# Issuing the later loads of x from ScalarE instead of SyncE in an RMSNorm + matmul kernel

## The chip, the cores and the metric

The kernel runs on one core of one Trainium2 chip. The metric is the device time of the whole kernel in microseconds (us), lower is better. The profiled span is about 2 us shorter than the time.

## The reference

```python
# x (16, 1024, 512) f32, weight (512, 768) f32, gamma (512,) f32, out (16, 1024, 768) f32
rms = np.sqrt(np.mean(x ** 2, axis=-1, keepdims=True) + eps)
return np.matmul(x / rms * gamma, weight)
```

The 16,384 rows are worked on as 128 tiles of 128 rows, in 64 pairs.

## The kernel before

Each tile of x is loaded in f32, cast to bf16 by GpSimd, transposed by TensorE (f32 words that hold two bf16), copied out of PSUM by VectorE and multiplied with the weights. ScalarE takes the sum of squares, and the result is scaled by 1/rms as it leaves PSUM: the first tile of a pair by ScalarE, the second by VectorE. Then it is stored. Two input buffers of 16 tiles and three output buffers of 8 tiles are used in turn.

```python
xin  = ctx.enter_context(tc.tile_pool(name="xin", bufs=2))    # 16 tiles each
outp = ctx.enter_context(tc.tile_pool(name="out", bufs=3))    # 8 tiles each
opsum = ctx.enter_context(tc.tile_pool(name="opsum", bufs=3, space=bass.MemoryType.PSUM))
# ... cut ...
def load(i):
    if i // XG not in x_tiles:
        x_tiles[i // XG] = xin.tile([P, XG, D], F32, name="xt")
    nc.sync.dma_start(out=held(x_tiles, XG, i, x_size[i]), in_=rows(x, i, x_size[i]))

def store(i):
    first, n = o_first[i], o_size[i]
    if i == first + n - 1:
        nc.sync.dma_start(out=rows(out, first, n), in_=held(o_tiles, OG, first, n))
# ... cut ...
for j in range(2, NP):
    load_until(2 * j + AHEAD)                  # AHEAD = 20 tiles
    if j + 3 < NP:
        cast(2 * j + 6, nc.gpsimd, 2)
    # ... squares of pair j + 2 on ScalarE, transposes of pair j + 2 fed between the matmuls ...
    for i, engine in ((2 * j, nc.scalar), (2 * j + 1, nc.vector)):
        a = accumulator()
        matmuls(i, a, range(K), feed)
        finish_tile(i, a, engine)              # scale into the output buffer, then store(i)
```

Loads of x and stores thus share SyncE's queue, in program order.

## Time and profile before

| | before |
|---|---|
| time, median of 3 | 211.08 us (210.78 to 211.16) |
| profiled span | 209.0 us |
| PE / ACT / VectorE / GpSimd busy | 96% / 72% / 52% / 32% |
| moved by DMA | 85.69 MB |
| pace of the matmuls from pair 6 on | 3.037 us a pair |

"Busy" is the share of the span.

### The profile page before, as it was taken

What the parts mean: (1) busy time and instruction counts of PE and PEld (TensorE: products, weight loads), DVE (VectorE), ACT (ScalarE), POOL (GpSimd) and SP (SyncE); (2) the same over time, 40 slices, a digit from 0 to 9 for tenths busy, and PEclk for the clock granted to TensorE, in tenths of its full rate; (3) what the DMA queues carried; (4) which work ended last, traced back from release to release, by engine and by line L of the source; (5) the groups of instructions that cost most, each with busy time, mean ns of one, the idle gap of its engine ahead of it and who ended that gap; (6) DMA issues with size and microseconds to landing.
All of it is one profiled execution on the core that took longest, in us unless ns stands there. A gap on an engine that the chain in (4) does not pass through costs nothing.

```text
span 209.0 us, 3534 instructions
## 1 busy us (share of the span) xinstructions
PE 201.6 (96%) x1298; PEld 137.9 (66%) x1298; DVE 109.0 (52%) x173; ACT 149.6 (72%) x359; POOL 67.0 (32%) x73
## 2 busy tenths in 40 slices
PE   7999999999999999999999999999999999999980
PEld 2466777666766776667766776667667766677640
DVE  0465654654565465456545644654564465456550
ACT  2689987787778778777877777787777778777640
POOL 1357532306331073213623062310633045230000
PEclk9999999999999999999999999999999999999999
DMA  6999999999999999999999999999999999899994
GB/s 231 392 430 422 408 395 436 424 414 439 431 458 411 412 442 425 447 411 437 428 448 419 423 423 442 433 433 417 428 442 447 405 441 414 381 386 386 383 374 182
DMA packets 7077, 85.69 MB, mean 410 GB/s; under 512 B 786, under 2 KB 916, under 8 KB 3476
## 3 DMA queue, kind: packets, MB, share of 16 engines
q1 hardware_dynamic: 7056, 85.46, 97.0%
q8 instruction: 10, 0.16, 0.3%
q14 instruction: 7, 0.06, 0.1%
q10 hardware_dynamic: 4, 0.00, 0.0%
HBM read 35.13 MB, written 50.33 MB: 409 GB/s over the span
## 4 chain that ended last, share of the span: by engine, by line
PE 91%; ACT 3%; DMA 2%; POOL 1%; DVE 1%; issue 0%; SPq 0%
PE ops L168 77%; PE tp L133 13%; DMA xt<-in_x_dram 2%; ACT jk L98 1%; ACT ot L150 1%; POOL xb L94 1%; ACT rms L102 0%; DVE xT L140 0%; PE ops L227 0%; DVE ot L152 0%; SPq L206 0%; DVE rstd L104 0%
## 5 line engine op out<-in xcount | busy, mean ns | idle before, releaser
L168 PE MATMUL ops<-w_bf,xT 128*128 128x256 bf16 (+1 forms) x1024 | 194.2, 326 | 0.3 <-DVE xT L140 0.3
L168 PEld LDWEIGHTS <-xT 128*128 128x128 bf16 x1024 | 100.0, 98 | 56.4 <-DVE xT L140 1.4
L94 POOL CAST xb<-xt 128x1024 bf16<-128x1024 f32 (+1 forms) x67 | 66.3, 1002 | 118.9 <-PE tp L133 72.9
L150 ACT ACTIVATE ot<-ops,rstd 128x768 f32<-128x768 f32 (+1 forms) x65 | 58.1, 894 | 47.2 <-PE ops L168 47.2
L140 DVE COPY xT<-tp 128x1024 bf16<-128x1024 bf16 (+1 forms) x67 | 44.7, 667 | 83.3 <-PE tp L133 83.0
L98 ACT ACTIVATE jk<-xt 128x512 bf16<-128x512 f32 x128 | 78.7, 619 | 0.7 <-DMA xt<-in_x_dram 0.7
L133 PE MATMUL tp<-ident_f,xb 128*128 128x128 f32 x256 | 68.9, 273 | 0.1
L152 DVE TENSOR_SCALAR ot<-ops,rstd 128x768 f32<-128x768 f32 (+1 forms) x65 | 64.5, 993 | 2.9 <-PE ops L168 2.9
L133 PEld LDWEIGHTS tp<-ident_f,xb 128*128 128x128 f32 x256 | 35.9, 141 | 3.8 <-POOL xb L94 0.7
L98 ACT ACTIVATION_READ_ACCUMULATOR jk<-xt 128x1 f32 x128 | 24.4, 191 | 0.0
L102 ACT ACTIVATE rms<-ssq,eps_sb 128x4 f32<-128x4 f32 (+3 forms) x35 | 10.4, 297 | 1.1
L104 DVE RECIPROCAL rstd<-rms 128x4 f32<-128x4 f32 (+3 forms) x35 | 5.9, 167 | 3.3 <-ACT rms L102 3.3
L227 PE MATMUL ops<-warm 128*128 128x512 bf16 x16 | 6.4, 561 | 1.2 <-DVE eps_sb L220 1.2
L227 PEld LDWEIGHTS <-warm 128*128 128x128 bf16 x16 | 1.9, 131 | 3.9 <-issue 2.5
L150 ACT ACTIVATE w_bf<-w_f,g_sb 128x768 bf16<-128x768 f32 x2 | 1.9, 936 | 3.6 <-DMA w_f<-in_weight_dram 3.6
L201 ACT ACT_TABLE_LOAD x1 | 1.3, 1283 | 1.3 <-PEq L330 1.3
L152 DVE TENSOR_SCALAR w_bf<-w_f,g_sb 128x512 bf16<-128x512 f32 (+2 forms) x3 | 1.4, 485 | 1.1 <-DMA w_f<-in_weight_dram 1.0
L241 DVE COPY g_sb<-tp 128x4 f32<-128x4 f32 x1 | 0.2, 162 | 3.1 <-PE tp L239 3.1
L239 PEld LDWEIGHTS tp<-ident_f,g_row 2*128 2x128 f32 x2 | 0.3, 200 | 0.8 <-issue 0.8
L218 DVE MEMSET warm<- 128x256 uint32 x1 | 0.3, 272 | 0.9 <-PEq L330 0.9
L239 PE MATMUL tp<-ident_f,g_row 2*128 2x2 f32 x2 | 0.4, 264 | 0.0
masks.py:199 POOL TENSOR_SCALAR_AFFINE_SELECT ident_f<-ident_f 128x128 f32<-128x128 f32 x1 | 0.3, 292 | 0.1
(6 smaller groups left out, 0.7 us busy)
## 6 DMA issues: line engine op xcount, KB each, us to landing
out_dram<-ot SPq DMA_DIRECT2D x12, 3072.0 KB, 16.3
xt<-in_x_dram SPq DMA_DIRECT2D x5, 4096.0 KB, 23.0
xt<-in_x_dram SPq DMA_DIRECT2D x3, 2048.0 KB, 19.4
out_dram<-ot SPq DMA_DIRECT2D x4, 1536.0 KB, 11.6
xt<-in_x_dram SPq DMA_DIRECT2D x4, 1024.0 KB, 13.2
out_dram<-ot SPq DMA_DIRECT2D x4, 768.0 KB, 10.4
out_dram<-ot SPq DMA_DIRECT2D x7, 384.0 KB, 11.2
w_f<-in_weight_dram SPq DMA_DIRECT2D x2, 768.0 KB, 5.9
```

The source lines that it names most:

```text
L94: engine.tensor_copy(out=xb_tiles[i // 2][:, i % 2:i % 2 + n, :], in_=held(x_tiles, XG, i, n))
L98: nc.scalar.activation(out=jk, in_=held(x_tiles, XG, i)[:, 0, :], func=AF.Square, accum_out=ssq)
L102: nc.scalar.activation(out=rms[:, :n], in_=ssq[:, :n], func=AF.Sqrt, scale=1.0 / D, bias=eps_sb)
L104: nc.vector.reciprocal(out=rstd[:, :n], in_=rms[:, :n])
L133: nc.tensor.transpose(out=tp_tiles[j][:, t, h, :], in_=words[:, lo:lo + P], identity=ident_f)
L140: nc.vector.tensor_copy(out=dst[:, t:t + n, :], in_=src[:, t:t + n, :])
L150: nc.scalar.mul(out=dst, in_=src, mul=r)
L152: nc.vector.tensor_single_scalar(out=dst, in_=src, scalar=r, op=mybir.AluOpType.mult)
L168: nc.tensor.matmul(out=acc[:, lo:hi], lhsT=xT_tiles[i // 2][:, i % 2, k // 2, :, k % 2], rhs=w_bf[:, k, lo:hi], start=(k == 0), stop=(k == ...
L201: nc.scalar.preload_act_table(AF.Sqrt)
L227: nc.tensor.matmul(out=spare[:, :WIDE], lhsT=warm[:, :P], rhs=warm, start=True, stop=True)
L239: nc.tensor.transpose(out=gp[:, c, :], in_=g_row[:, :, c], identity=ident_f[:2, :2])
```

## The change

The intent is that loads and stores no longer stand behind each other in one queue: the loads from tile 32 on (two of 2048 KB, five of 4096 KB) are issued by ScalarE on its own queue, stores stay on SyncE's.

```diff
-        nc.sync.dma_start(out=held(x_tiles, XG, i, x_size[i]), in_=rows(x, i, x_size[i]))
+        queue = nc.sync if i < 2 * XG else nc.scalar
+        queue.dma_start(out=held(x_tiles, XG, i, x_size[i]), in_=rows(x, i, x_size[i]))
```

## The prediction

> **What bounds the kernel now.** I read the page of the kernel before first: busy shares, chain, costliest groups. The span is 209.0 us.
>
> ```profile
> PE 201.6 (96%) x1298; PEld 137.9 (66%) x1298; DVE 109.0 (52%) x173; ACT 149.6 (72%) x359; POOL 67.0 (32%) x73
> ...
> q1 hardware_dynamic: 7056, 85.46, 97.0%
> ...
> PE 91%; ACT 3%; DMA 2%; POOL 1%; DVE 1%; issue 0%; SPq 0%
> ...
> L168 PE MATMUL ops<-w_bf,xT 128*128 128x256 bf16 (+1 forms) x1024 | 194.2, 326 | 0.3 <-DVE xT L140 0.3
> ```
>
> The chain that ended last is 91% PE, and the matmuls of L168 waited 0.3 us in all. In the trace a new pair of tiles starts every 3.037 us from pair 6 (27.72 us) to pair 62 (197.78 us), without a break. So TensorE sets the end. But one queue, q1, is busy for 97% of the span: I had to ask how close the transfers are to taking over.
>
> In the steady part, 8 pairs take 8 x 3.037 = 24.3 us and need one load of 4096 KB and two stores of 3072 KB (the page's DMA issues): 4.194 + 2 x 3.146 = 10.49 MB, or 432 GB/s. Each transfer reports one completion for each of 16 DMA engines, and the last of the 16 counts. For the big loads that last one is at 72.72, 97.28, 121.53, 145.71 and 169.93 us: the last gaps are 24.25, 24.18 and 24.22 us, so the laggard engines also run at about 433 GB/s without a pause. Both sides go at the same pace, with a standing backlog: the load issued at 98.77 lands 22.76 us later, though the store in front of it landed 9.70 us earlier (111.83). So 13 of its 22.8 us were spent behind stores. That is what the change attacks.
>
> Then the timelines of SyncE's issues, GpSimd's casts and ScalarE around one load:
>
> ```profile
> 47.39 0.33 SPq L165 DMA_DIRECT2D out_dram<-ot  x1
> 49.84 0.34 SPq L83 DMA_DIRECT2D xt<-in_x_dram  x1
> 59.54 12.48 SPq L165 DMA_DIRECT2D out_dram<-ot  x2
> ...
> 72.87 3.01 POOL L94 CAST xb<-xt 128x1024 bf16<-128x1024 f32 x3 [7.80 <-DMA xt<-in_x_dram]
> ...
> 49.59 0.19 ACT L98 ACTIVATION_READ_ACCUMULATOR jk<-xt 128x1 f32 x1
> ...
> 53.73 0.90 ACT L150 ACTIVATE ot<-ops,rstd 128x768 f32<-128x768 f32 x1 [0.58 <-PE ops L168]
> 54.53 0.62 ACT L98 ACTIVATE jk<-xt 128x512 bf16<-128x512 f32 x1
> ...
> 75.79 0.62 ACT L98 ACTIVATE jk<-xt 128x512 bf16<-128x512 f32 x1
> ...
> 76.31 0.14 PEld L133 LDWEIGHTS tp<-ident_f,xb 128*128 128x128 f32 x1
> ```
>
> The load of tiles 48 to 63 goes out at 49.84, as soon as ScalarE's last square of tile 31 (ends 49.78) frees the buffer. It lands at 72.72, GpSimd starts the cast of pair 24 at 72.87, after 7.80 us of idleness, and ends it at 73.91. TensorE loads pair 24 for its transposes at 76.31, ScalarE squares it from 75.79. So GpSimd's 43.9 us of waiting for x costs nothing: the load has a **slack** of 76.31 - 73.91 = 2.4 us (2.3 to 2.6 at the later loads). Its deadline is a landing by about 75.1.
>
> **What the Trainium skill says.** "DMA: Bandwidth & Descriptors", section "Issuing engines are not separate DMA queues": transfers issued by different engines run on the same 16 DMA engines and interleave, and only sequencer time is saved. So no bandwidth is added. Section "Queues, rings and completion order" of that page: SyncE and ScalarE own one row of rings each, and each DMA engine round-robins between the rows it has work for, a packet at a time. The trace before can't confirm this, since nearly all went over q1; it does show packets of 32 KB for loads and 24 KB for stores. In "Where 436 GB/s comes from" the ceiling is put at 435 GB/s; the 432 GB/s above agrees, so I expect no faster stream than now.
>
> **The change, part by part.** Nothing is added in bytes or arithmetic. Comparing instruction orders, seven load issues leave SyncE and stand on ScalarE, each just after an output scaling of L150; the stores keep their order on SyncE.
>
> 1. ScalarE pays 7 issues x 0.34 us (SyncE's duration for one) = 2.4 us. ScalarE idles 0.58 or 0.92 us in each pair (the bracketed waits for PE), so each issue hides. On the path: 0.
>
> 2. The issue comes later. The condition that puts the load of tile 48 in iteration 15 was only a queue position on SyncE, which waited there from iteration 13 for the buffer. ScalarE reaches it after scaling tile 28, at about 54.55 instead of 49.84: 4.7 us lost. The loads of tiles 32 and 40 would go at 30.3 and 42.3 (before: 29.6 and 35.6); their slack is large, and they no longer stand behind stores.
>
> 3. The load no longer queues behind 13 us of stores but shares with them. The total backlog is conserved: 12.8 us of work (on the laggard engines) stood before the load at 50.2 us, so about 8.1 us of stores are left at 54.9, and the next store adds 7.3 us at 59.9. There is store work for the whole of the load, which gets 32/(32+24) = 4/7 if packets alternate. Its 4.194 MB take 9.7 us alone (431 GB/s), so 9.7 x 7/4 = 17.0 us. With some 1.4 us of start and completion (the first weight load took 3.0 us to its first landing for 1.8 us of data), it lands at 54.9 + 1.4 + 17.0 = 73.3 (estimate), against 72.7 before and the deadline 75.1. In sum it loses 4.7 us at issue and gains 4.1 in the queue: 0 on the path. If the shares go by bytes, half and half, it takes 19.5 us and lands at 75.8: TensorE waits 0.7 us.
>
> 4. Stores are squeezed instead. The store issued at 72.0 shares with the load of tile 64, now issued near 79.2. With 8.1 us of store work left when the load becomes active (80.6) and 3/7 of the engines, 7.3 us of it is done when the load ends (97.6), and the store lands at about 98.4 instead of 87.3. Its buffer is one of three: tile 56 needs it when its matmuls end, half a pair after pair 28 starts at 94.53, that is at 96.05. ScalarE would wait some 2.3 us there. TensorE has three accumulators; tile 59 needs tile 56's at 99.1, so the slack is 99.1 - 96.05 - 0.9 (scaling) = 2.1 us. Cost: 0 to 0.5 us in each of about five periods.
>
> 5. The end. The total of bytes ahead of the last store is the same, TensorE ends as before plus its waits. 0.
>
> Sum: 0.0 + 0 to 0.7 us of waits in up to five periods. Every such wait lets the transfers catch up (a period longer by 0.5 us takes 0.5 us off the backlog), so later periods cost less. I choose 0.7 us in total: 211.08 + 0.7 = 211.8.
>
> **The rivals.** *The load becomes late.* If stores get more than half, the landing slips past 75.1 and the chain shows GpSimd and x again and again. From a landing to the next issue on ScalarE is about 4 us (75.1 to 79.2), so a period is the load's latency plus 4: over 20.3 us of latency each further us is lost in full, until the 8 us backlog has drained. That could come to 4 to 8 us: 215 to 219. For it speaks the later issue and a slack of 2.4 us, against it the larger load packets. *The output buffer becomes the wait* (part 4): ScalarE held by stores, then TensorE by accumulators. For it: a store latency near 26 us against 24 us of buffer time. Against: 2.1 us of slack in the accumulators. 212 to 214. *Mixing reads and writes changes the rate.* A loss of 3% makes a period 25.0 us, 0.7 us over PE's pace: over five or six periods 4 us, less what slack hides: 213 to 215. A gain of 3% buys nothing. *Faster because the load skips the queue*: the wait removed is GpSimd's, which is hidden; TensorE's only breaks lie before 25 us, ahead of the change. At best 210.7.
>
> **Range and chances.** TensorE's unbroken pace rules out a real gain: faster by over 2% gets 0.02. Two margins of about 2 us each are nearly used up, so a small loss is likelier than none; a loss of over 4.2 us needs 0.8 us in each of five periods, against the draining of the backlog, or a lower mixed rate: 0.13. Within 2%: 0.85. The range is 210.6 to 215.5, longer upward.
>
> **What would show it.** Right: loads of tile 48 on issued by ScalarE near 54.5 and every 24.3 us, landing 18 to 20 us later; GpSimd's idle spell of 8 us unchanged or shorter by little; stores next to a load at 22 to 26 us; the matmuls still 3.037 us a pair; a few ScalarE waits on stores at the first tile of an output group. Wrong: matmuls or transposes waiting for casts in every period (step 3 fell), ScalarE and DVE waiting for stores for many us (step 4), or the GB/s of the middle slices off the present 410 to 450 (step 3's conserved rate). A time under 210 would mean that I misread what binds.

## More of the kernel before

The prediction shows the page's lines. Two views that it did not show matter for what follows. The first is SyncE's own waits, with what was waited for, the total in us, the count and the longest:

```profile
SPq L165 <- DVE ot L152: 161.4, 22, 11.8
SPq L83 <- ACT jk L98: 10.1, 5, 2.1
SPq L344 <- DMA out_dram<-ot: 3.5, 1, 3.5
```

SyncE mostly waits for finished output tiles (no harm: it has nothing else to do), and in five cases for the squares that free an input buffer. L344 is the end of the program: after the last issue SyncE waits 3.5 us for the last store to land. The second view is its last issues (start, duration in us, times):

```profile
203.45 0.97 SPq L311 DMA_DIRECT2D out_dram<-ot  x2
```

They are over at 204.42.

## The result, and the profile after

The changed kernel takes 210.9 us (median of 4, 210.55 to 211.19), the kernel before, run with it, 210.93 us (210.43 to 211.16 over 4). The ratio is 1.000, with a 95% interval of 0.998 to 1.0019. A ratio here is the mean time of one kernel's fast runs over that of the other's of the same rounds, so it is not quite the ratio of the medians. Executions over 1.5% slower than the fastest of the same kernel are left out of the means. Where I give a difference in us below, it is (ratio - 1) x 210.9.

The forecast loss of 0.7 us did not come. The page of the changed kernel: busy shares, queues, chain, and two groups of instructions (busy us, mean ns | idle before, releaser).

```profile
PE 199.9 (96%) x1273; PEld 137.3 (66%) x1298; DVE 109.0 (52%) x173; ACT 149.8 (72%) x359; POOL 66.6 (32%) x73
...
q1 hardware_dynamic: 6048, 60.30, 68.9%
q10 hardware_dynamic: 1012, 25.17, 28.4%
...
PE 79%; DMA 13%; ACT 3%; POOL 1%; issue 1%; DVE 1%; SPq 0%; POOLq 0%
...
L134 PE MATMUL tp<-ident_f,xb 128*128 128x128 f32 x256 | 69.0, 273 | 1.3 <-POOL xb L95 1.2
L134 PEld LDWEIGHTS tp<-ident_f,xb 128*128 128x128 f32 x256 | 35.8, 141 | 6.1 <-POOL xb L95 3.0
```

The last two groups in the kernel before:

```profile
L133 PE MATMUL tp<-ident_f,xb 128*128 128x128 f32 x256 | 68.9, 273 | 0.1
...
L133 PEld LDWEIGHTS tp<-ident_f,xb 128*128 128x128 f32 x256 | 35.9, 141 | 3.8 <-POOL xb L94 0.7
```

25.17 MB, the seven loads, now go over q10. (PE's count is lower because 25 matmul records are missing from this trace; the weight loads, 1298 as before, are all there.) The chain has 13% DMA in it, and TensorE's transposes now wait for GpSimd's casts. The chain in order of time shows where (start us, us, what):

```profile
53.89 22.10 DMA xt<-in_x_dram
...
76.14 1.05 POOL xb L95
77.19 0.04 issue
77.23 0.33 PE tp L134
```

The chain passes through one load, that of tile 48. This does not mean that 22 us were lost: TensorE worked beside nearly all of them. Pair 23's transposes start at 73.64, and at 3.037 us a pair those of pair 24 were due at 76.68; they start at 77.23, 0.55 us late. ScalarE's and GpSimd's timelines around this load:

```profile
53.88 0.90 ACT L151 ACTIVATE ot<-ops,rstd 128x768 f32<-128x768 f32 x1 [0.59 <-PE ops L169]
53.89 0.33 ACTq L84 DMA_DIRECT2D xt<-in_x_dram  x1
...
76.14 4.98 POOL L95 CAST xb<-xt 128x1024 bf16<-128x1024 f32 x5 [10.92 <-DMA xt<-in_x_dram]
```

Issue at 53.89 (before: 49.84), last completion at 75.99 (72.72), GpSimd idle for 10.92 us (7.80) and then five casts in a row to catch up (three). The slack of 2.4 us is used up and overdrawn once. The later loads cost next to nothing: from pair 6's transposes to pair 63's TensorE takes 172.41 us, against 171.80 before, so all of its loss is 0.61 us, practically at pair 24.

And yet the end does not move. SyncE's last issues, and its wait at the end, after the change:

```profile
204.22 0.96 SPq L312 DMA_DIRECT2D out_dram<-ot  x2
```

```profile
SPq L345 <- DMA out_dram<-ot: 2.5, 1, 2.5
```

The last issue is 0.77 us later (0.15 of it were there before pair 6), the final wait for the store is 1.0 us shorter. That is where the loss went. The completions of the last stores tell why. Each transfer reports 16 times. In the kernel before, 13 of the last store's 16 had come by 206.48, the others at 207.12, 207.81 and 207.98. The slowest completions of the last five stores are 205.16, 206.09, 207.01, 207.65 and 207.98: 0.93 us apart for the stores of 384 KB, then less for the smaller ones, which is 423 GB/s (0.393 MB in 0.93 us) with no gap. So a few DMA engines are still working off a queue when TensorE is done. After the change the slowest ones are 204.92, 205.87, 206.82, 207.43 and 207.76: the same sequence, 0.2 us earlier, though TensorE was later. The first completions of the last store did follow TensorE: 206.32 before, 207.09 after. Only the last ones did not. (Even spacing alone does not tell the slow engines from the others: the first completions of the 384 KB stores are 0.96 to 1.0 us apart too.)

This gives the theory that I tested, the **laggard theory**: at the end the kernel waits for the last few DMA engines, which have had an unbroken queue since the start; TensorE has a margin of 1 to 1.5 us, and what it loses within that margin is free. It also says that the order of transfers cannot matter for the end, as long as the bytes are the same and the laggards never run dry. The **rival** is the prediction's own: TensorE sets the end, and the equality is chance.

### The profile page after: what moved, and what is told of

Its sections match the earlier page's. It is cut to its first block, busy times and chain, and to the rows that moved or that the text cites. A ratio compares the mean times of both kernels' runs of the same rounds, so it can differ in the third digit from the quotient of the medians.

```text
span 208.8 us, 3499 instructions
## 1 busy us (share of the span) xinstructions
PE 199.9 (96%) x1273; PEld 137.3 (66%) x1298; DVE 109.0 (52%) x173; ACT 149.8 (72%) x359; POOL 66.6 (32%) x73
## 3 DMA queue, kind: packets, MB, share of 16 engines
q10 hardware_dynamic: 1012, 25.17, 28.4%
## 4 chain that ended last, share of the span: by engine, by line
PE 79%; DMA 13%; ACT 3%; POOL 1%; issue 1%; DVE 1%; SPq 0%; POOLq 0%
PE ops L169 67%; DMA xt<-in_x_dram 13%; PE tp L134 12%; ACT jk L99 1%; POOL xb L95 1%; ACT ot L151 1%; ACT rms L103 0%; DVE xT L141 0%; PE ops L228 0%; DVE ot L153 0%; SPq L207 0%; POOLq L95 0%; DVE rstd L105 0%
## 5 line engine op out<-in xcount | busy, mean ns | idle before, releaser
L169 PE MATMUL ops<-w_bf,xT 128*128 128x512 bf16 (+1 forms) x999 | 192.8, 325 | 1.5 <-DVE xT L141 0.3
L151 ACT ACTIVATE ot<-ops,rstd 128x768 f32<-128x768 f32 (+1 forms) x65 | 58.1, 893 | 47.2 <-PE ops L169 46.6
L228 PE MATMUL ops<-warm 128*128 128x512 bf16 x16 | 5.4, 482 | 1.2 <-DVE eps_sb L221 1.2
## 6 DMA issues: line engine op xcount, KB each, us to landing
out_dram<-ot SPq DMA_DIRECT2D x4, 768.0 KB, 10.9
```

The source lines that it names most:

```text
L151: nc.scalar.mul(out=dst, in_=src, mul=r)
L169: nc.tensor.matmul(out=acc[:, lo:hi], lhsT=xT_tiles[i // 2][:, i % 2, k // 2, :, k % 2], rhs=w_bf[:, k, lo:hi], start=(k == 0), stop=(k == ...
L228: nc.tensor.matmul(out=spare[:, :WIDE], lhsT=warm[:, :P], rhs=warm, start=True, stop=True)
```

## The experiments

All ran with five rounds beside the kernel before (extra_load left four executions on record, drop2_before five, the others six), and the results are correct unless I say otherwise. "TensorE's path" is the time from the start of pair 6's transposes to that of pair 63's (before: 171.80 us); the final wait is that of SyncE at the end of the program, in the profiled run.

| kernel | ratio to before | TensorE's path, us | final wait, us |
|---|---|---|---|
| before | 1 | 171.80 | 3.5 |
| changed | 1.000 | 172.41 | 2.5 |
| pe_plus2 | 1.0003 | 172.44 | 3.0 |
| pe_plus8 | 1.0069 | 174.38 | 2.0 |
| extra_load | 1.0106 | 171.79 | 5.8 |
| drop_store | 0.9949 | 171.78 | 2.4 |
| after_earlier, fast runs | 0.9998 | (profile is of a slow run) | |
| after_earlier_4out | 0.9996 | 171.79 | 3.1 |
| after_plus8 | 1.0101 | 174.97 | 2.2 |

### pe_plus2 and pe_plus8: TensorE late on purpose

Needless matmuls, each a group of its own that the real first one overwrites, in the kernel before.

```diff
     def matmuls(i, acc, ks, feed=None):
+        for _ in range(2 if i == 60 else 0):       # pe_plus8: 8
+            for lo, hi in ((0, WIDE), (WIDE, O)):
+                nc.tensor.matmul(out=acc[:, lo:hi], lhsT=xT_tiles[i // 2][:, i % 2, 0, :, 0],
+                                 rhs=w_bf[:, 0, lo:hi], start=True, stop=True)
         for k in ks:
```

> The kernel before with two needless k=0 matmul pairs (each 0.32 us) at tile 60: TensorE is 0.65 us late from there on, much as in the changed kernel. Laggard theory (the last DMA engines drain an unbroken queue until 207.98 us, and TensorE has about 1.5 us in hand, because the 13 fast engines land the last store at 206.40): the last issue moves from 204.42 to about 205.07, the last landing stays near 208.0, time 0.0 to +0.15 us. Rival (TensorE sets the end, and the equality of the two kernels is chance): +0.65 us.

Measured: ratio 1.0003 (0.9983 to 1.0022), that is +0.06 us, while TensorE's path grew by 0.64 us. The rival's +0.65 us is outside the interval. SyncE's final wait:

```profile
SPq L347 <- DMA out_dram<-ot: 3.0, 1, 3.0
```

It shrank by 0.5 us. TensorE can lose 0.6 us in this kernel without any effect.

> The kernel before with eight needless k=0 matmul pairs (2.6 us) at tile 60. Laggard theory: the 1.5 us in hand are used up, then TensorE sets the end: last issue 207.0, landing 2.0 us later at 209.0, time +1.0 us. Rival (TensorE sets the end): +2.6 us.

Measured: 1.0069 (1.0052 to 1.0087), +1.45 us, for 2.58 us on TensorE's path. By these two, 1.13 us were free and the rest counted. The laggard theory had said +1.0 (1.5 us free), the rival +2.6. The figure mixes a mean of executions with one trace. In the two profiled executions alone the last issues end 3.46 us later (207.88 against 204.42; 0.87 of it were there before pair 6, at 24.03 us against 23.16) and the span is 1.95 us longer, so 1.5 us were free. The margin is there, of 1.1 to 1.5 us. That TensorE now sets the end is seen directly: all 16 completions of the last store lie within 0.16 us (209.77 to 209.93), where the kernel before had 1.66. The last issues and the final wait:

```profile
206.91 0.97 SPq L314 DMA_DIRECT2D out_dram<-ot  x2
```

```profile
SPq L347 <- DMA out_dram<-ot: 2.0, 1, 2.0
```

About 2 us is thus what the last small store takes when hardly anything stands before it.

### extra_load: more bytes that nobody waits for

```diff
+        scratch = singles.tile([P, 4 * D], F32)
...
             load_until(2 * j + AHEAD)
+            if j == 50:
+                nc.sync.dma_start(out=scratch, in_=x[:4 * P, :].rearrange("(p t) d -> p (t d)", t=4))
```

> The kernel before with one more load of 1 MB into a scratch tile that nobody reads, on SyncE's queue at iteration 50, after the last load of x. No engine waits for it; stores behind it land up to 2.4 us later, inside their 24 us of buffer time. Laggard theory: 1.05 MB at 432 GB/s are 2.4 us more of queue, and all of it shows at the end: +2.4 us with TensorE's matmuls unmoved. Rival (TensorE sets the end): 0, at most +0.3 us.

Measured: 1.0106 (1.009 to 1.0123), +2.24 us, with TensorE's path unchanged (171.79 us). The 1 MB shows almost in full, as the laggard theory says; the rival had 0 to 0.3. All of it is in the final wait:

```profile
SPq L347 <- DMA out_dram<-ot: 5.8, 1, 5.8
```

### drop_store: fewer bytes

```diff
-        if i == first + n - 1:
+        if i == first + n - 1 and first != 40:
```

> The kernel before without the store of tiles 40 to 47 (3072 KB; the result is wrong there on purpose). TensorE's work is unchanged. Laggard theory: the queue is 7.3 us shorter, the laggards catch up before the end, the last store (issued at 204.4) lands 2.0 us later at 206.4 on all engines: -1.5 us, and the spread of the last store's 16 completions falls from 1.7 us to under 0.3. Rival (TensorE sets the end): 0 to -0.3 us.

The result is wrong (one store of eight tiles is missing). Measured: 0.9949 (0.9933 to 0.9964), -1.08 us, TensorE's path unchanged.

```profile
SPq L344 <- DMA out_dram<-ot: 2.4, 1, 2.4
```

The direction is the laggard theory's; the size is not quite its -1.5 us. Fifteen of the 16 engines now complete the last stores together, but one is still 0.6 us behind: of the next-to-last issue, fifteen are in by 206.26 and the last is at 206.84. Its queue was 7.3 us shorter, more than any spread among one transfer's 16 completions in the kernel before (at most 5.5 us), and it is still late: I conclude that this engine is also slower in the last phase, where only stores run. It still sets the end here, so the 1.08 us are not the whole of what TensorE has in hand; they are no contradiction to the 1.1 to 1.5 us of pe_plus8.

### drop2_before and drop2_after: both kernels with the queue out of the way

```diff
-        if i == first + n - 1:
+        if i == first + n - 1 and first not in (40, 72):
```

> The kernel before without the stores of tiles 40 to 47 and 72 to 79 (wrong there on purpose): 14.6 us of queue less, so that even the slowest DMA engine, which one dropped store left 0.6 us behind, has caught up at the end. Laggard theory: last issue near 204.3, last landing 2.1 us later on all engines, time -1.0 to -1.5 us against the kernel before, now set by TensorE. Rival (TensorE always set the end): -1.0 us was something else; no further change is told.

> The changed kernel with the same two stores dropped. With the queue out of the way, TensorE's loss in the changed kernel must show. Laggard theory: the 0.6 us wait before pair 24 is still there (both dropped stores come after it) and the time is 0.5 to 0.8 us above that of the kernel before with the same stores dropped. Rival (the changed kernel lost nothing on TensorE that counts): equal within 0.2 us.

Both results are wrong. Measured: 0.9944 (0.9932 to 0.9956) for the kernel before with both stores dropped, -1.18 us, and 0.9961 (0.9943 to 0.9979) for the changed one. The first is within what was expected, but the slowest engine had not caught up, as it should have: fifteen completions of the last store are in by 206.70, the last comes at 207.26. So dropping a second store bought hardly more than the first, and what is left of the lag is hardly an old queue. The difference is 0.36 us and lies between what the two theories said; the intervals overlap. The executions of the changed kernel split, 209.39, 209.50 and 209.65 against 210.27, 210.47 and 210.61, those of the other lie within 209.37 to 209.88. In the profiled pair TensorE's path is 172.18 against 171.79 us. The dropped stores give the load of tile 64 and the later ones more room, but not that of tile 48. I take this pair as inconclusive.

### after_plus8: the changed kernel with TensorE in charge

The needless matmuls of pe_plus8, put into the changed kernel, ask the same question with a correct result and all bytes.

> The changed kernel with the eight needless matmul pairs (2.6 us) at tile 60 that made the kernel before 1.45 us slower (ratio 1.0069) and put TensorE in charge of the end. If the changed kernel loses some 0.6 us on TensorE before pair 24 in most executions, which the queue hides as long as the laggards set the end, it must show here: ratio to before 1.0085 to 1.0105 (212.7 to 213.1 us). If that loss isn't there or is rare: 1.0069, about 212.4.

Measured: 1.0101 (1.0075 to 1.0127), +2.13 us, against +1.45 for pe_plus8. The ratio lies in the range told for a real loss, and its interval leaves out 1.0069, though only just, and pe_plus8's own interval overlaps it. TensorE's path is the firmer evidence: 174.97 us against 174.38, 0.59 us longer, with pair 24 again 0.5 us late. (The profiled spans can't be set side by side: pair 6 starts at 22.91 us here and at 24.03 in pe_plus8.) I read the two together as a real loss of about 0.6 us in the changed kernel, which shows in the time once TensorE sets the end.

### after_earlier: the load one pair sooner

```diff
-    AHEAD = 20
+    AHEAD = 22
```

> The changed kernel with AHEAD 22 for 20: ScalarE reaches each big load one pair (3.04 us) earlier, near 50.9 instead of 53.9 for tile 48. It should land near 73 instead of 76.0, before GpSimd's deadline of 75.1, so TensorE's 0.6 us wait before pair 24 goes away and its last work is as early as in the kernel before. Laggard theory: the end stays, ratio to the kernel before 0.998 to 1.002. Rival (TensorE sets the end of the changed kernel): 0.6 us less than the changed kernel, near 210.3, ratio 0.997 or less.

Measured: three executions at 210.27, 210.95 and 211.07 us (ratio 0.9998, 0.9983 to 1.0013) and three at 213.5 to 213.99. The granted clock is the same in all six (0.994 to 0.997), so this is not a throttled state. The fast ones are as the laggard theory says. The profile fell on a slow one; its load of tile 48 landed at 73.23, close to the 73 expected, and pair 24 was on time (76.59 us, 3.04 after pair 23). What failed was elsewhere. ScalarE's waits, and one of them in the timeline:

```profile
ACT ot L151 <- PE ops L169: 44.3, 53, 3.6
ACT ot L151 <- DMA out_dram<-ot: 5.6, 2, 3.6
```

```profile
173.32 0.90 ACT L151 ACTIVATE ot<-ops,rstd 128x768 f32<-128x768 f32 x1 [3.57 <-DMA out_dram<-ot]
```

ScalarE waits for a store to leave its output buffer, and holds up TensorE through the accumulators: TensorE's path is 174.03 us here, 2.2 us over the kernel before. Four stores beside loads took 25.6 to 28.3 us to land, more than the 24 us until the buffer is wanted again. This is the second rival of the prediction, brought out by issuing loads sooner.

### after_earlier_4out: the same with a fourth output buffer

```diff
-    outp = ctx.enter_context(tc.tile_pool(name="out", bufs=3))
+    outp = ctx.enter_context(tc.tile_pool(name="out", bufs=4))
```

> The changed kernel with AHEAD 22 and four output buffers for three. With three, half of its executions were 3 us slower, and in the slow one that was profiled ScalarE waited 5.6 us for stores that landed 25.6 to 28.3 us after issue, more than the 24 us until their buffer is wanted. Output-buffer theory: with four buffers a store has 36 us, ScalarE's wait for stores is 0 in the profile, all executions lie within 210.2 to 211.3, ratio to before 0.998 to 1.002. Rival (the slow executions come from the DMA engines, not from the buffer): some executions of 213.5 to 214 remain.

Measured: six executions from 210.2 to 211.62 us (the kernel before: 210.7 to 211.78), all fast, ratio 0.9996 (0.997 to 1.0022). ScalarE waits for no store, and TensorE's path is 171.79 us, as in the kernel before. The slow executions were the output buffer's doing. This kernel has both repairs, the load in time and the stores with room, and it is still no faster than the kernel before: what it would save is saved on the engine that does not set the end.

### skew_store: an attempt to take work off the laggards

```diff
-            nc.sync.dma_start(out=rows(out, first, n), in_=held(o_tiles, OG, first, n))
+            for lo, hi in ((0, 104), (104, P)) if first == 40 else ((0, P),):
+                nc.sync.dma_start(out=rows(out, first, n)[lo:hi], in_=held(o_tiles, OG, first, n)[lo:hi])
```

> The kernel before with the one store of tiles 40 to 47 split into 104 partitions (if that runs on 13 engines, 8 partitions each) and 24 partitions (12 engines, 2 each), so that up to three engines carry nothing of it. It asks whether the laggards are those three. If they are: they win 7.3 us, the others lose 1.8 us of a lead of 1.5 to 3.7 us, and the time falls by 0.5 to 1.3 us. If the laggards are others: they carry a quarter more of this store, and the time rises by 1.8 us.

Measured: 1.0323 (1.0295 to 1.035), +6.8 us, over three times what either case allowed. The profile is of the one execution that counts as slow (219.97 us; the fast ones took 216.61 to 218.79), so its times are a rough guide. The two pieces reported 13 and 12 completions of data, so they did run on 13 and 12 engines. But together they took some 15 us instead of 7 (the median completion is at 93.70 for the load in front of them, at 104.27 and 108.50 for the pieces). From 94 to 110 us the data rate was 275 GB/s, with the DMA engines 97% busy; in the kernel before it was 435. The next load landed late, and GpSimd waited for it:

```profile
POOL xb L94 <- DMA xt<-in_x_dram: 13.9, 1, 13.9
```

This split cost far more than the share of any engine explains, for a reason that I did not find, so the run says nothing on which engines lag. I found no version that beats both kernels: the changed ones tie with the kernel before, and all that there is to win on the side of the DMA engines is the margin to TensorE's end, 1.1 to 1.5 us, under one per cent.

## Why the prediction was right or wrong

The measured 210.9 us is within 2% of the kernel before and inside the range, but the forecast loss of 0.7 us is wrong in time. On TensorE it is nearly right (0.61 us), and that is luck: it came once, by a route that the prediction had not named.

**What binds.** "So TensorE sets the end" is the statement that failed, and with it step 5, "TensorE ends as before plus its waits". I had shown that both sides run at the same pace and then gave the end to TensorE, because the chain does. The chain ends with the last instruction of an engine; the store that lands afterwards is not in it. pe_plus2, extra_load and drop_store show the opposite: 0.64 us on TensorE cost 0.06 us, 1 MB more cost 2.24, and 3 MB less gained 1.08. TensorE has 1.1 us in hand by the means (2.58 - 1.45 in pe_plus8, 3.17 - 2.13 in after_plus8), 1.5 by the profiled pair of pe_plus8; the changed kernel's 0.61 us is within it.

**Step 1** held: an issue takes 0.33 us on ScalarE and hides; ScalarE's waits for matmuls are 46.6 us in all against 47.2.

**Step 2** held but for 0.66 us: the issue goes out at 53.89, together with the scaling of tile 28 (53.88), not after it.

**Step 3** had the share right for this load and one term wrong. Between 56 and 73 us the load's queue moved 4.10 MB and the stores' 3.15 MB, 57% or 4/7 (58 to 63% for the four later loads, from 82 to 98, 106 to 122, 131 to 146 and 156 to 171 us). The term "1.4 us of start and completion" was the mistake; it came to 4.8 (75.99 - 54.22 - 17.0). It was taken from a load with nothing before it, up to the first of its 16 completions, and even there 3.0 - 1.8 is 1.2. That load's first packets start 0.6 us after its issue (1.12 to 1.74 us). The load of tile 48 was issued by 54.22 and its first packet starts at 57.58: 3.4 us before the DMA engines turn to the new queue (3.1 to 3.6 for all seven loads). Why they take so long is not shown. The slowest engine did the rest: 15 of the 16 completions had come by 74.50, the last came at 75.99. So the load landed at 75.99 instead of 73.3 and missed the deadline of 75.1. The cost on TensorE, 0.6 us, is what I had given to the half-and-half case, by another route.

**Step 4** was too dark for the changed kernel. The store issued near 72.0 landed at 93.1, not 98.4, and ScalarE's only wait put down to a store is of 0.6 us:

```profile
ACT ot L151 <- DMA out_dram<-ot: 0.6, 1, 0.6
```

It stands at 47.81 us, before the big loads, and is no longer than ScalarE's usual wait for TensorE (0.58), so it cost nothing. The late start of the load explains 2 us of the difference, in which stores had the engines to themselves. The other 3 us I cannot assign. The mechanism itself is real: after_earlier fell into it.

**The sum.** I expected up to five waits that shrink, and it was one (0.55 us), then none. The later loads land with less delay (21.1, 20.5, 20.6 and 21.1 us after 21.8). That may be the draining that I argued, but the last one has grown again, and no run was made to show it.

**The signs.** Three of those that I named failed: the loads took 20.5 to 21.8 us and not 18 to 20, GpSimd's idle spell grew from 8 to between 9.6 and 10.9 us, and the stores beside the big loads took 19 to 21 us, below the 22 to 26 told.

**The rivals.** The conserved rate held: from 26 to 178 us the data rate (last column, after share of DMA) is 429 GB/s before and 428 after.

```profile
26.00:178.00 152.00, 152.00 (x1003) 106.51 (x1001) 83.34 (x126) 113.48 (x275) 51.34 (x50) 1.00 1.01 429
```

```profile
26.00:178.00 152.00, 150.56 (x979) 105.92 (x998) 82.81 (x126) 113.61 (x275) 50.77 (x51) 1.00 1.01 428
```

What stays open: which DMA engines lag and why, and whether an engine's lag at the end is an old queue or its own slower pace (drop_store and drop2_before speak for some of each). The trace gives completions without the engine's number, and skew_store failed to tell.

## What to carry to other kernels

When two resources run at the same pace, look at what is outstanding after the last instruction before you name the one that sets the end: here a last small store that took 3.5 us instead of 2 was the sign that some DMA engines were behind. Moving transfers to another queue changed their order here and not their rate (429 and 428 GB/s); it helps only if somebody on the path was waiting for the order. A load on a queue of its own was not immediate beside full DMA engines (3.4 us to its first packet), and what it gained was taken from the stores (one beside a load landed at 93.1 us instead of 87.3), so check the output buffers' time too.

## What the Trainium skill lacked or had wrong

- "DMA: Bandwidth & Descriptors", section "Queues, rings and completion order", says that the engines alternate between queues packet by packet. It gives no shares of the bytes: here packets of 32 KB against 24 KB gave the first big load 57% (4.10 of 7.24 MB between 56 and 73 us) and the later ones 58 to 63%.
- Its section "Latency and other measured facts" gives about 0.6 us to the first byte of a transfer issued by SyncE or ScalarE, which fits the program's first load (1.12 to 1.74 us), and no figure for a start beside a full queue: here it was 3.4 us from issue to the first packet (54.22 to 57.58 us), on a queue that was itself all but empty. The same section guesses that two DMA engines are usually slow because of the rings of descriptors that GpSimd's transfers use, and takes this not to concern transfers of SyncE and ScalarE. Here GpSimd issues none, and three of the 16 completions of the last store come 0.6 to 1.5 us after the other thirteen (207.12, 207.81, 207.98 against 206.48); the trace does not tell which engines these are.
- I found no page with the cost of an uneven split: one store of 3 MB in pieces of 104 and 24 partitions cost 6.8 us, with 275 GB/s for 435 while it ran.
